# Next MLP block's rows turned from the fifth product on into a third pool of tiles, its sums split into stages, and some evictions and block outputs issued in later steps

## The chip, the cores and the metric

The kernel runs on one core of a Trainium2 chip. The metric is the time on the device in microseconds (us), the median of the runs shown.

## The reference, cut to what matters

The reference is one layer of a hybrid decoder, in float32, for 2048 prompt rows and 64 sample rows of width 1024. A token mixer (attention, a state space model and a short convolution side by side) comes first and is not touched by the change. Behind it stands the MLP:

```python
        h = rms_norm(x, norm_mlp_pre[l])
        f = jnp.square(jax.nn.relu(h @ w_mlp_up[l])) @ w_mlp_down[l]
        x = x + rms_norm(f, norm_mlp_post[l])
```

The first product goes from 1024 to 4096 columns, the second back.

## The kernel before, in words

The MLP stage is the code from line 1566 on; in the profiled execution it runs from about 1345 us to the end of the span. The 2112 rows are done in three blocks of 704 (`BT`), and each block has two halves of 352 rows (`HT`), called t = 0 and 1 where they are read, 1 and 2 where they are written. Rows are cut into three pieces `TP` of 128, 128 and 96.

**Products.** Both matrix products of a block are done by a scheme of the Strassen kind: each is cut in two along rows, inner dimension and columns, and seven products of combined quarters replace eight. `UP_ORDER` is 1, 2, 6, 7, 5, 3, 4 and `DOWN_ORDER` is 1, 2, 7, 4, 5, 6, 3; the numbers name the products, so that "the fifth and sixth product" of the change are the numbers 5 and 6 of the down order. Quarters of the weights were combined earlier and lie in HBM. A product runs over eight steps (`jj`), a step holds two column tiles j. Every operand is split into a high part (a cast to fp32r) and a low part (the rest), and `mm3` issues three matmuls for each pair: high by high, high by low, low by high. An up step has 24 matmuls of 128x352, a down step 18 of 128x512.

**The operands.** The weight of a step is loaded by SyncE's queue (`wraw4`), its high half is made by ScalarE (`whi4`, line 1604), and its low half (`wlo4`) by GpSimd in up steps and by VectorE in down steps (`w_split`). The moving operand is split by `s_pair`: ScalarE makes `shi` (line 1612), VectorE makes `slo`. The pool s4 holds seven such pairs. VectorE's and GpSimd's operations are recorded by a helper, so that all of them have line 137 in the profile; TensorE's have line 118, its transposes 122.

**Inputs of up.** `Half` loads normalised rows (`xt4`) from the scratch xn_d on SyncE's queue, turns them by transposes on TensorE into `pq` banks, and ScalarE copies each with the gain into a `q` tile (line 1638): eight for each half, `q11`, `q12` for the first and `q21`, `q22` for the second, four tiles in each. `up_sums` makes the combined inputs of products 6, 7, 5 and 3 from them on VectorE, four operations for each of four tiles c, three of them TENSOR_TENSOR (`s3` = q11 − q21, then q21 − q22, then q11 becomes q21 − q11) and one SCALAR_TENSOR_TENSOR (q12). It begins when the fourth pair of product 2 has been emitted. `next_block`, a generator that the main loop advances, is started at down product 6, step 2, for the block after.

**Outputs.** `up_out` evicts a bank of an up product on VectorE or ScalarE (line 1701) into the inner tiles `X`, which `relu2` squares on ScalarE (lines 1694, 1695). `down_out` evicts a bank of a down product into the `y1` and `y2` tiles (three operations on a bank in product 6, two in product 5). `square` sums the squares of y on ScalarE (`jkf`, line 1805); `mlp_out` makes the norm's factor (`ssf`, `rstd`) on GpSimd, scales y on VectorE, and adds it to the result by a DMA on GpSimd's queue.

**Order of the work.** The kernel is emitted step by step in the main loop (line 1846 on), but a list scheduler (`schedule_with_timeline_sim=True`) places the instructions on each engine's queue after that, by its own simulated times; only `tc.issue_after(V.last)` pins an operation behind VectorE's last one. Pools of tiles: f4 has 64 of 128x352, r4 8, t4 2.

Of the kernel before, what the change touches and what calls it, by code (L numbers as in the profile page):

```python
# [10 lines left out]
F32 = mybir.dt.float32  # L11
# [3 lines left out]
ALU = mybir.AluOpType  # L15
# [4 lines left out]
P = 128  # L20
# [5 lines left out]
TT = S + TS  # L26
# [17 lines left out]
HT = 352  # L44
BT = 2 * HT
# [99 lines left out]
def hybrid_layer(ctx: ExitStack, tc: tile.TileContext, I, O, stage=9):  # L145
    nc = tc.nc
    V, A, G, PE, SP = Last(nc.vector), nc.scalar, Last(nc.gpsimd), TimedPE(nc.tensor), Last(nc.sync)
# [81 lines left out]
    def sb(name, bufs, side=None):  # L229
        return tc.tile_pool(name=name, bufs=bufs, side=side, reuse_waits="tile")  # L230
# [13 lines left out]
    streams = []  # L244
# [106 lines left out]
    p1l, p1r, p3, p4, psm, ppo = (ExitStack() for _ in range(6))  # L351
# [7 lines left out]
    psT = p4.enter_context(psb("psT", 2))  # L359
# [773 lines left out]
    class Tok:  # L1133
# [436 lines left out]
    e4 = s4 = w4 = r4 = f4 = y4 = t4 = psD = None  # L1570
# [37 lines left out]
    def s_pair(src):  # L1608

        hi = s4.tile([P, HT], F32R, name="shi", tag="s")  # L1610
        lo = s4.tile([P, HT], F32R, name="slo", tag="s")
        A.copy(hi, src)  # L1612
        V.tensor_sub(lo, src, hi.bitcast(F32))
        return hi, lo

    class Half:
# [13 lines left out]
        def turn(self, ps, tag):  # L1630

            self.q = [], []
            for k in range(KC):
                pt = ps.tile([P, 512], F32, name=f"pq{k}", tag=tag)
                for xt, a, n in self.xs:
                    PE.transpose(pt[:, a:a + n], xt[:n, k * P:(k + 1) * P], ident[:n, :n])
                q = (r4 if self.t == 0 else f4).tile([P, HT], F32, name="q", tag="f")
                A.activation(q, pt[:, :HT], AF.Copy, scale=vec[:, V_MLP + k:V_MLP + k + 1])
                self.q[k // 4].append(q)
                yield 1.0  # L1640
# [46 lines left out]
    Y = {}  # L1687

    def f_tile(t, f, j):
        X[t, f, j] = (r4 if (t, f) == (2, 2) and j >= 12 else f4).tile([P, HT], F32, name=f"x{t}{f}", tag="f")  # L1690
        return X[t, f, j]

    def relu2(x, sign):
# [28 lines left out]
    def up_sums(b):  # L1722

        (q11, q12), (q21, q22) = halves[b, 0].q, halves[b, 1].q
        while len(up_s.get((b, 2), [])) < 4:
# [10 lines left out]
        src.update({(b, 6): q11, (b, 7): s3, (b, 5): q21, (b, 3): q12, (b, 4): q22})  # L1736

    src = {}

    def up_split(b, i, cs):  # L1740
        up_s.setdefault((b, i), []).extend(s_pair(src[b, i][c]) for c in cs)

    down_s = {}

# [62 lines left out]
    def mlp_out(b, t, p, last=False):  # L1807
# [14 lines left out]
        for t1, t2 in ((t0, min(t0 + n, S)), (max(t0, S), t0 + n)):  # L1822
            if t1 < t2:
                G.dma_start(y_rows(t1, t2 - t1), y[t1 - t0:t2 - t0], accum_op=ALU.add)

    def second_half(b):

        h = halves[b, 1] = Half(b, 1, XT if b else [(y4, "y")])
        h.rows()
        yield 10.0  # L1830
        yield from h.turn(psT, "tr")
        yield from up_sums(b)

    def next_block(b):
        h = halves[b, 0] = Half(b, 0, XT)
        h.rows()
        yield 16.0
        yield from h.turn(psT, "tr")
# [6 lines left out]
    for at, (kind, b, i, jj) in enumerate(steps):  # L1845
        if at + 4 < len(steps):
            w_load(at + 4)
        while nsplit[0] < len(steps) and nsplit[0] <= at + (2 if idle_y(nsplit[0]) else 1):
            w_split(nsplit[0])
            nsplit[0] += 1  # L1850
        order = UP_ORDER if kind == "u" else DOWN_ORDER
        nxt = steps[at + 2] if at + 2 < len(steps) else None

        if kind == "u" and jj == NJ // 2 - 2 and i != UP_ORDER[-1]:
            ni = UP_ORDER[UP_ORDER.index(i) + 1]
            if ni == 6:
                while (b, 6) not in src:
                    advance(min(streams, key=lambda st: st[1]))
            up_split(b, ni, (0, 1, 2))
        if kind == "d" and i == DOWN_ORDER[-1] and jj == NJ // 2 - 1 and (b + 1, 1) in src:  # L1860
            up_split(b + 1, 1, (0, 1, 2))

        two = steps[at + 1] if at + 1 < len(steps) else None
        if two is not None and two[0] == "d" and kind == "d":
            for j2 in range(2):
                down_split(two[1], two[2], 2 * two[3] + j2)
        if kind == "u":
            hi, lo = wts.pop(at)
            s = up_s[b, i]
            for j2 in range(2):  # L1870
                ps = bank()
                for c in range(4):
                    ws = slice(2 * P * c + P * j2, 2 * P * c + P * j2 + P)
                    mm3(ps[:, :HT], hi[:, ws], lo[:, ws], *s[c], c == 0, c == 3)
                up_out(i, 2 * jj + j2, ps)
        else:
            hi, lo = wts.pop(at)
            if jj == 0:
                banks = [bank() for _ in TP]
            for j2 in range(2):  # L1880
                j = 2 * jj + j2
                s = down_s.pop((b, i, j))
                ws = slice(512 * j2, 512 * j2 + 512)
                for p, (a, n) in enumerate(TP):
                    mm3(banks[p][:n], s[0][:, a:a + n], s[1][:, a:a + n], hi[:, ws], lo[:, ws], j == 0, j == NJ - 1)
            if jj == NJ // 2 - 1:
                for p in range(len(TP)):
                    down_out(i, p, banks[p])
        if two is not None and two[0] == "d" and kind == "u":
            for j2 in range(2):  # L1890
                down_split(two[1], two[2], 2 * two[3] + j2)
        if kind == "u" and jj == NJ // 2 - 1 and i != UP_ORDER[-1]:
            up_split(b, UP_ORDER[UP_ORDER.index(i) + 1], (3,))
        if kind == "d" and i == DOWN_ORDER[-1] and jj == NJ // 2 - 1 and b + 1 < TT // BT:
            while (b + 1, 1) not in src:
                advance(min(streams, key=lambda st: st[1]))
            have = len(up_s.get((b + 1, 1), []))
            up_split(b + 1, 1, range(have, 4))
        if kind == "d":
            end, last = jj == NJ // 2 - 1, b == TT // BT - 1  # L1900
            if i == 2 and end:
                for p in range(len(TP)):
                    square(1, p, 1)
                    if last:
                        o = Y[1, p][:TP[p][1], :512]
                        V.tensor_mul(o, o, g4[:TP[p][1], :512])
            if i == 6 and end:
                for p in range(len(TP)):
                    for d in (1, 2):
                        square(2, p, d)  # L1910
            if i == 3 and not end and 1 <= jj <= len(TP):
                mlp_out(b, 2, jj - 1)
            if i == 3 and end:
                for p in range(len(TP)):
# [48 lines left out]
```

## Time and profile before

| what | value |
|---|---|
| runs | 2792.34, 2794.55 and 2804.75 us, median 2794.55 |
| profiled execution | 2796.83 us, of which the span is 2794.9 |
| mean granted clock of TensorE in it | 0.968 |
| TensorE matmuls busy | 2588.7 us, 93% of the span |
| VectorE, ScalarE, GpSimd busy | 55%, 48%, 39% |

The busy shares are means over the whole program. In the rows of a timeline, the first two numbers are the start and the duration in us, and the brackets hold the idle time of that engine ahead of the row and what ended it. In a group, busy time and the mean in ns stand behind the bar. The clock is a share of full speed.

### The profile page before, as it was taken

Reading aid. Unit: us, or ns where it says so; the run is one execution under the profiler, and the core shown is the slowest. Engines: PE = TensorE matmul, PEld = TensorE weight load, DVE = VectorE, ACT = ScalarE, POOL = GpSimd, SP = SyncE. Lnnn points to the kernel's source line nnn. Section 1 sums busy time; section 2 is a strip of 40 time slices with the busy share of each in tenths; the row PEclk is TensorE's granted clock in tenths of the full one; section 3 lists DMA queues with packets and bytes.
Section 4 is the critical chain, followed back from the end, with each engine's and each line's share of the span. In section 5 each row is a group of like instructions: output and inputs, shape, how many; then the busy total and the mean of one; then the engine's idle time right before and its main releaser. Section 6 shows DMA issues by size and latency. Waiting matters only on the chain. (4 is left out here: it accounts for less than half of the span.)

```text
span 2794.9 us, 40722 instructions
## 1 busy us (share of the span) xinstructions
PE 2588.7 (93%) x14329; PEld 2186.8 (78%) x14329; DVE 1531.4 (55%) x2994; ACT 1327.7 (48%) x2776; POOL 1078.8 (39%) x1008
## 2 busy tenths in 40 slices
PE   7998889999899878999899999999999999999996
PEld 6897777877877755567799877689987779998775
DVE  4555436456456465554164466844546684445676
ACT  4534334435436333334446654453764455385434
POOL 4545445444354543334567300166610016661002
PEclk9999989999999989999999999999999999999998
DMA  7777998777677549878777545574434456443443
GB/s 210 218 185 224 276 254 228 199 218 213 173 207 205 152 149 287 266 227 260 233 233 212 140 157 171 145 218 146 166 128 151 149 146 197 162 163 128 128 146 92
DMA packets 426260, 528.26 MB, mean 189 GB/s; under 512 B 65482, under 2 KB 326130, under 8 KB 421448
## 3 DMA queue, kind: packets, MB, share of 16 engines
q1 hardware_dynamic: 411352, 483.45, 54.5%
q0 software_dynamic: 14704, 42.21, 9.2%
q8 instruction: 113, 1.85, 0.3%
q14 instruction: 91, 0.75, 0.1%
HBM read 447.90 MB, written 178.19 MB: 224 GB/s over the span
## 5 line engine op out<-in xcount | busy, mean ns | idle before, releaser
L137 POOL TENSOR_TENSOR wlo<-wraw,whi 128x512 fp32r<-128x512 f32 (+2 forms) x359 | 670.7, 1899 | 555.0 <-ACT whi L417 288.4
L1604 ACT CAST whi<-wraw 128x1024 fp32r<-128x1024 f32 x336 | 351.7, 1049 | 341.4 <-PE pm L118 274.3
L118 PE MATMUL pm<-slo,whi 128*128 128x352 f32 x1344 | 437.9, 327 | 16.1 <-DVE slo L137 10.0
L118 PE MATMUL pm<-shi,wlo 128*128 128x352 f32 x1344 | 433.1, 328 | 7.6 <-POOL wlo L137 7.5
L118 PE MATMUL pm<-shi,whi 128*128 128x352 f32 x1344 | 438.2, 326 | 0.0
L118 PE MATMUL pm<-wlo,shi 128*128 128x512 f32 (+1 forms) x1008 | 400.1, 397 | 1.9 <-ACT shi L1612 1.7
L118 PE MATMUL pm<-whi,shi 128*128 128x512 f32 (+1 forms) x1008 | 398.4, 395 | 0.0
L118 PE MATMUL pm<-whi,slo 128*128 128x512 f32 (+1 forms) x1008 | 338.1, 399 | 17.6 <-DVE slo L137 17.6
L137 DVE TENSOR_TENSOR wlo<-wraw,whi 128x1024 fp32r<-128x1024 f32 (+1 forms) x169 | 206.2, 1220 | 198.1 <-ACT whi L1604 189.1
L118 PE MATMUL pj<-lo,whi 128*128 128x512 f32 (+1 forms) x720 | 273.1, 380 | 17.0 <-ACT xr L631 8.1
L118 PEld LDWEIGHTS pm<-slo,whi 128*128 128x128 f32 x1344 | 256.0, 191 | 19.9 <-DVE slo L137 11.2
L118 PE MATMUL pj<-hi,whi 128*128 128x512 f32 (+1 forms) x720 | 263.1, 365 | 0.0
L118 PEld LDWEIGHTS pm<-shi,wlo 128*128 128x128 f32 x1344 | 255.1, 191 | 9.2 <-POOL wlo L137 8.9
L118 PE MATMUL pj<-hi,wlo 128*128 128x512 f32 (+1 forms) x720 | 262.1, 365 | 0.0
L137 POOL TENSOR_TENSOR ssf<-ssf 128x1 f32<-128x1 f32 (+1 forms) x18 | 6.6, 369 | 647.1 <-ACT jkf L1805 647.0
L118 PEld LDWEIGHTS pm<-shi,whi 128*128 128x128 f32 x1344 | 256.0, 191 | 0.2
L137 DVE TENSOR_TENSOR x<-pm,x 128x352 f32<-128x352 f32 x240 | 123.4, 521 | 222.5 <-PE pm L118 222.4
L118 PEld LDWEIGHTS pm<-whi,slo 128*128 128x128 f32 (+1 forms) x1008 | 179.7, 181 | 76.0 <-DVE slo L137 26.3
L118 PEld LDWEIGHTS pm<-wlo,shi 128*128 128x128 f32 (+1 forms) x1008 | 182.4, 181 | 60.4 <-ACT shi L1612 8.7
L118 PEld LDWEIGHTS pm<-whi,shi 128*128 128x128 f32 (+1 forms) x1008 | 182.0, 181 | 51.2
L1612 ACT CAST shi<-x 128x352 fp32r<-128x352 f32 x288 | 136.9, 484 | 155.0 <-DVE x L137 102.8
L137 DVE TENSOR_TENSOR slo<-x,shi 128x352 fp32r<-128x352 f32 x288 | 157.1, 554 | 35.6 <-ACT shi L1612 30.5
(324 smaller groups left out, 4887.3 us busy)
## 6 DMA issues: line engine op xcount, KB each, us to landing
wraw<-in_w_in SPq DMA_DIRECT2D x192, 256.0 KB
wraw<-u_d SPq DMA_DIRECT2D x96, 512.0 KB
wraw<-d_d SPq DMA_DIRECT2D x96, 512.0 KB
wraw<-in_w_mlp_up SPq DMA_DIRECT2D x72, 512.0 KB
wraw<-in_w_mlp_down SPq DMA_DIRECT2D x72, 512.0 KB
u_d<-in_w_mlp_up POOLq DMA_DIRECT2D x64, 256.0 KB, 5.6
d_d<-in_w_mlp_down POOLq DMA_DIRECT2D x64, 256.0 KB, 7.3
out_s_k<-in_cache_attn_k SPq DMA_DIRECT2D x8, 2040.0 KB
```

The source lines that it names most:

```text
L118: return self.eng.matmul(out, lhsT, rhs, **kw)
L137: out = f(*args, **kw)
L1604: A.copy(hi, raw)
L1612: A.copy(hi, src)
```

## The change

It does four things, all in the MLP stage.

1. The pool f4 shrinks from 64 to 48 tiles, and a new pool v4 has 16. The second half's `q` tiles come from v4, and so do twelve of the inner tiles X(2,2) (the other four stay in r4).
2. `next_block` starts at down product 5, step 4, and turns the second half ahead of the first.
3. `up_sums` is cut into stages, and `s3` is no longer among them: first q21 − q22, after the pairs of product 1 q11 = q21 − q11, after those of product 2 q12. `s3` is formed in `up_split` just before product 7 splits it, by SCALAR_TENSOR_TENSOR into a t4 tile.
4. At the end of down products 5 and 6 the first bank is evicted at once, the evictions of the second and third (with the squares of y2) go onto a list `late`, of which one is issued in each following step. The finish of y1 at a block's end (square and `mlp_out`) goes onto the same list, except in the last block. `mlp_out` of y2 comes in steps 2 to 4 of product 3 instead of 1 to 3.

```diff
-    f4 = p4.enter_context(sb("f4", 64, "left"))
+    f4 = p4.enter_context(sb("f4", 48, "left"))
+    v4 = p4.enter_context(sb("v4", 16, "left"))
...
-                q = (r4 if self.t == 0 else f4).tile([P, HT], F32, name="q", tag="f")
+                q = (r4 if self.t == 0 else v4).tile([P, HT], F32, name="q", tag="f")
...
-        while len(up_s.get((b, 2), [])) < 4:
-            yield 1.0
-        s3 = []
-        for c in range(4):
-            s3.append(f4.tile([P, HT], F32, name="s3", tag="f"))
-            with tc.issue_after(V.last):
-                V.tensor_sub(s3[c], q11[c], q21[c])
-                V.tensor_sub(q21[c], q21[c], q22[c])
-                V.tensor_sub(q11[c], q21[c], q11[c])
-                V.scalar_tensor_tensor(q12[c], q12[c], -1.0, q11[c], op0=ALU.mult, op1=ALU.subtract)
-            yield 3.0
+        yield from each(lambda c: V.tensor_sub(q21[c], q21[c], q22[c]))
+        while len(up_s.get((b, 1), [])) < 4:
+            yield 1.0
+        yield from each(lambda c: V.tensor_sub(q11[c], q21[c], q11[c]))
+        src.update({(b, 6): q11, (b, 5): q21, (b, 4): q22})
+        while len(up_s.get((b, 2), [])) < 4:
+            yield 1.0
+        yield from each(lambda c: V.scalar_tensor_tensor(q12[c], q12[c], -1.0, q11[c], op0=ALU.mult,
+                                                         op1=ALU.subtract))
...
+            if i == 7:
+                a = t4.tile([P, HT], F32, name="s3", tag="t")
+                V.scalar_tensor_tensor(a, src[b, 6][c], -1.0, src[b, 4][c], op0=ALU.mult, op1=ALU.subtract)
...
     def next_block(b):
-        h = halves[b, 0] = Half(b, 0, XT)
-        h.rows()
-        yield 16.0
-        yield from h.turn(psT, "tr")
-        src[b, 1], src[b, 2] = h.q
-        yield from second_half(b)
+        yield from half(b, 1)
+        yield 6.0
+        yield from half(b, 0)
+        src[b, 1], src[b, 2] = halves[b, 0].q
+        yield from up_sums(b)
...
+        if late:
+            late.pop(0)()
...
                 for p in range(len(TP)):
-                    down_out(i, p, banks[p])
+                    if i in (5, 6) and p:
+                        late.append(lambda i=i, p=p, ps=banks[p]: end_tile(i, p, ps))
+                    else:
+                        end_tile(i, p, banks[p])
...
-        if kind == "d" and i == 6 and jj == 2 and b + 1 < TT // BT:
+        if kind == "d" and i == 5 and jj == 4 and b + 1 < TT // BT:
             stream(next_block(b + 1))
```

What the scheduler makes of it is seen in the queues. Three places follow, all on VectorE, in block 0's down products or block 1's up products.

The end of up product 2 of block 1, before; x11 are evictions of product 2, the q and s3 rows are the sums, and the slo of shi_19108 belongs to the fourth tile of product 6:

```order
L137 TENSOR_TENSOR slo_19031<-q_18102,shi_19030 128x352
L137 TENSOR_TENSOR x11_19007<-pm_18994,x12_18632 128x352
L137 TENSOR_TENSOR s3_19011<-q_18150,q_18638 128x352
L137 TENSOR_TENSOR q_18638<-q_18638,q_18834 128x352
L137 TENSOR_TENSOR q_18150<-q_18638,q_18150 128x352
L137 TENSOR_TENSOR x11_19047<-pm_19034,x12_18675 128x352
L137 SCALAR_TENSOR_TENSOR q_18319<-q_18319,q_18150 128x352
L137 TENSOR_TENSOR x11_19064<-pm_19051,x12_18690 128x352
L137 TENSOR_TENSOR x11_19087<-pm_19074,x12_18717 128x352
L137 TENSOR_TENSOR slo_19109<-q_18150,shi_19108 128x352
```

And with the change, where slo of shi_19103 is that fourth tile's:

```order
L137 TENSOR_TENSOR x11_18925<-pm_18912,x12_18595 128x352
L137 SCALAR_TENSOR_TENSOR q_18397<-q_18397,q_18373 128x352
L137 TENSOR_TENSOR x11_18949<-pm_18936,x12_18617 128x352
L137 TENSOR_TENSOR x11_18966<-pm_18953,x12_18632 128x352
L137 SCALAR_TENSOR_TENSOR q_18403<-q_18403,q_18379 128x352
L137 TENSOR_TENSOR x11_18990<-pm_18977,x12_18654 128x352
L137 TENSOR_TENSOR x11_19007<-pm_18994,x12_18669 128x352
L137 TENSOR_TENSOR x11_19042<-pm_19029,x12_18707 128x352
L137 TENSOR_TENSOR x11_19059<-pm_19046,x12_18722 128x352
L137 TENSOR_TENSOR x11_19082<-pm_19069,x12_18744 128x352
L137 TENSOR_TENSOR slo_19104<-q_18379,shi_19103 128x352
```

The tensor sums have left the place, and one SCALAR_TENSOR_TENSOR (q12) stands for each two evictions; what moved stands at the start of product 1 and of product 2.

The end of down product 6 of block 0, before; y rows are evictions, x12 forms the operands of product 3, and slo of shi_17961 is product 3's first:

```order
L137 TENSOR_TENSOR y2_17150<-pm_17718,y2_17150 128x512 x2
L137 TENSOR_TENSOR y1_16580<-pm_17718,y1_16580 128x512
L137 TENSOR_TENSOR y2_17152<-pm_17719,y2_17152 128x512 x2
L137 TENSOR_TENSOR y1_16582<-pm_17719,y1_16582 128x512
L137 TENSOR_TENSOR y2_17154<-pm_17720,y2_17154 96x512 x2
L137 TENSOR_TENSOR y1_16584<-pm_17720,y1_16584 96x512
L137 TENSOR_TENSOR wlo4_18016<-wraw4_17881,whi4_18015 128x1024
L137 SCALAR_TENSOR_TENSOR x12_14048<-x12_14048,x11_14402 128x352
L137 TENSOR_TENSOR slo_17962<-x12_14020,shi_17961 128x352
```

And with the change, where slo of shi_18006 is product 3's first:

```order
L137 TENSOR_TENSOR y2_17153<-pm_17725,y2_17153 128x512 x2
L137 TENSOR_TENSOR y1_16583<-pm_17725,y1_16583 128x512
L137 TENSOR_TENSOR y2_17155<-pm_17726,y2_17155 128x512 x2
L137 TENSOR_TENSOR y1_16585<-pm_17726,y1_16585 128x512
L137 SCALAR_TENSOR_TENSOR x12_14051<-x12_14051,x11_14399 128x352
L137 TENSOR_TENSOR y2_17157<-pm_17727,y2_17157 96x512 x2
L137 TENSOR_TENSOR y1_16587<-pm_17727,y1_16587 96x512
L137 TENSOR_TENSOR wlo4_18045<-wraw4_17914,whi4_18044 128x1024
L137 SCALAR_TENSOR_TENSOR x12_14087<-x12_14087,x11_14446 128x352
L137 TENSOR_TENSOR slo_18007<-x12_14023,shi_18006 128x352
```

One x12 row has moved ahead of the third bank's evictions, and another ahead of the first slo; no eviction has moved behind that slo.

The end of block 0 and start of up product 1 of block 1, before; slo of shi_18650 belongs to product 2, and the y1 rows are the last evictions of the block:

```order
L137 TENSOR_TENSOR slo_18363<-q_18102,shi_18362 128x352
L137 TENSOR_TENSOR slo_18367<-q_18150,shi_18366 128x352
L137 TENSOR_TENSOR slo_18651<-q_18198,shi_18650 128x352
L137 TENSOR_TENSOR y1_16580<-pm_18029,y1_16580 128x512
L137 TENSOR_TENSOR y1_16582<-pm_18030,y1_16582 128x512
L137 TENSOR_TENSOR y1_16584<-pm_18031,y1_16584 96x512
L137 TENSOR_TENSOR slo_18655<-q_18238,shi_18654 128x352
L137 TENSOR_TENSOR slo_18659<-q_18278,shi_18658 128x352
```

And with the change, where slo of shi_18682 is product 2's:

```order
L137 TENSOR_TENSOR slo_18415<-q_18373,shi_18414 128x352
L137 TENSOR_TENSOR slo_18419<-q_18379,shi_18418 128x352
L137 TENSOR_TENSOR y1_16583<-pm_18066,y1_16583 128x512
L137 TENSOR_TENSOR slo_18683<-q_18385,shi_18682 128x352
L137 TENSOR_TENSOR y1_16585<-pm_18067,y1_16585 128x512
L137 TENSOR_TENSOR y1_16587<-pm_18068,y1_16587 96x512
L137 TENSOR_TENSOR q_17750<-q_17750,q_17912 128x352
L137 TENSOR_TENSOR slo_18687<-q_18391,shi_18686 128x352
```

The first eviction of y1 has moved ahead of product 2's first slo, and the first sum (q_17750) has come in behind the third eviction.

More of the change, by code (lines that the diff above doesn't have):

```diff
@@ L1569, in hybrid_layer @@
     UP_ORDER, DOWN_ORDER = (1, 2, 6, 7, 5, 3, 4), (1, 2, 7, 4, 5, 6, 3)
-    e4 = s4 = w4 = r4 = f4 = y4 = t4 = psD = None
+    e4 = s4 = w4 = r4 = v4 = f4 = y4 = t4 = psD = None
     shifts = [(nm, src, b) for b in range(NB) for nm, src in (("s_k", "cache_attn_k"), ("s_v", "cache_attn_v"))]
@@ L1689, in f_tile @@
     def f_tile(t, f, j):
-        X[t, f, j] = (r4 if (t, f) == (2, 2) and j >= 12 else f4).tile([P, HT], F32, name=f"x{t}{f}", tag="f")
+        pool = f4 if (t, f) != (2, 2) else v4 if j < 12 else r4
+        X[t, f, j] = pool.tile([P, HT], F32, name=f"x{t}{f}", tag="f")
         return X[t, f, j]
@@ L1724, in up_sums, with each @@
         (q11, q12), (q21, q22) = halves[b, 0].q, halves[b, 1].q
+        def each(f):
+            for c in range(4):
+                with tc.issue_after(V.last):
+                    f(c)
+                yield 3.0
+        yield from each(lambda c: V.tensor_sub(q21[c], q21[c], q22[c]))
[3 more added lines that the diff above has]
+        src.update({(b, 6): q11, (b, 5): q21, (b, 4): q22})
         while len(up_s.get((b, 2), [])) < 4:
             yield 1.0
-        s3 = []
-        for c in range(4):
-            s3.append(f4.tile([P, HT], F32, name="s3", tag="f"))
-            with tc.issue_after(V.last):
-                V.tensor_sub(s3[c], q11[c], q21[c])
-                V.tensor_sub(q21[c], q21[c], q22[c])
-                V.tensor_sub(q11[c], q21[c], q11[c])
-                V.scalar_tensor_tensor(q12[c], q12[c], -1.0, q11[c], op0=ALU.mult, op1=ALU.subtract)
-            yield 3.0
-        src.update({(b, 6): q11, (b, 7): s3, (b, 5): q21, (b, 3): q12, (b, 4): q22})
+        yield from each(lambda c: V.scalar_tensor_tensor(q12[c], q12[c], -1.0, q11[c], op0=ALU.mult,
+                                                         op1=ALU.subtract))
+        src[b, 3] = q12
     src = {}
     def up_split(b, i, cs):
-        up_s.setdefault((b, i), []).extend(s_pair(src[b, i][c]) for c in cs)
+        while (b, 6 if i == 7 else i) not in src:
+            advance(min(streams, key=lambda st: st[1]))
+        for c in cs:
+            if i == 7:
+                a = t4.tile([P, HT], F32, name="s3", tag="t")
+                V.scalar_tensor_tensor(a, src[b, 6][c], -1.0, src[b, 4][c], op0=ALU.mult, op1=ALU.subtract)
+            else:
+                a = src[b, i][c]
+            up_s.setdefault((b, i), []).append(s_pair(a))
     down_s = {}
@@ L1824, in mlp_out, with end_tile, half @@
                 G.dma_start(y_rows(t1, t2 - t1), y[t1 - t0:t2 - t0], accum_op=ALU.add)
+    def end_tile(i, p, ps):
+        down_out(i, p, ps)
+        for t, d in {2: [(1, 1)], 6: [(2, 1), (2, 2)]}.get(i, []):
+            square(t, p, d)
+    def half(b, t):
+        h = halves[b, t] = Half(b, t, XT if b else [(y4, "y")])
+        h.rows()
+        yield 12.0
+        yield from h.turn(psT, "tr")
     def second_half(b):
-        h = halves[b, 1] = Half(b, 1, XT if b else [(y4, "y")])
-        h.rows()
-        yield 10.0
-        yield from h.turn(psT, "tr")
+        yield from half(b, 1)
         yield from up_sums(b)
     def next_block(b):
-        h = halves[b, 0] = Half(b, 0, XT)
-        h.rows()
-        yield 16.0
-        yield from h.turn(psT, "tr")
-        src[b, 1], src[b, 2] = h.q
-        yield from second_half(b)
+        yield from half(b, 1)
+        yield 6.0
+        yield from half(b, 0)
+        src[b, 1], src[b, 2] = halves[b, 0].q
+        yield from up_sums(b)
+    late = []
     nsplit = [1]
@@ L1855, in hybrid_layer @@
             ni = UP_ORDER[UP_ORDER.index(i) + 1]
-            if ni == 6:
-                while (b, 6) not in src:
-                    advance(min(streams, key=lambda st: st[1]))
             up_split(b, ni, (0, 1, 2))
@@ L1900, in hybrid_layer, with finish @@
             end, last = jj == NJ // 2 - 1, b == TT // BT - 1
-            if i == 2 and end:
+            if i == 2 and end and last:
                 for p in range(len(TP)):
[L1903 to L1912, printed above, removed]
+                    o = Y[1, p][:TP[p][1], :512]
+                    V.tensor_mul(o, o, g4[:TP[p][1], :512])
+            if i == 3 and not end and 2 <= jj < 2 + len(TP):
+                mlp_out(b, 2, jj - 2)
             if i == 3 and end:
-                for p in range(len(TP)):
+                def finish(p, b=b, last=last):
                     square(1, p, 2)
                     mlp_out(b, 1, p, last)
-        if kind == "d" and i == 6 and jj == 2 and b + 1 < TT // BT:
+                for p in range(len(TP)):
+                    if last:
+                        finish(p)
+                    else:
+                        late.append(lambda p=p, f=finish: f(p))
+        if kind == "d" and i == 5 and jj == 4 and b + 1 < TT // BT:
             stream(next_block(b + 1))
```

1 line of the change is left out of this document (added).

## The prediction

> **What bounds the kernel now.** I read the page first, then the waits of TensorE in the MLP stage, which is the only stage that the change touches (about 1345 us of the span to its end), then windows of 25 us there, and last the timelines of the engines around each hole. The page's first row says what sets the time:
>
> ```profile
> PE 2588.7 (93%) x14329; PEld 2186.8 (78%) x14329; DVE 1531.4 (55%) x2994; ACT 1327.7 (48%) x2776; POOL 1078.8 (39%) x1008
> ```
>
> TensorE is the bound and the change gives it the same matmuls as before. So the time can only change by holes in TensorE, and by the clock after them. Two entries of what TensorE waits for between 1345 and 2795 us:
>
> ```profile
> PE pm L118 <- DVE slo L137: 27.6, 14, 3.7
> PE pq L122 <- DMA xt<-xn_d: 3.6, 3, 2.0
> ```
>
> The 27.6 us are 14 waits for a low half (slo) from VectorE. The windows say where the long holes are (columns: stretch, length, busy time of PE, PEld, DVE, ACT, POOL, granted clock):
>
> ```profile
> 1825.00:1850.00 25.00, 20.55 (x116) 19.46 (x116) 8.15 (x9) 13.15 (x27) 18.26 (x17) 0.93 0.65 160
> 1875.00:1900.00 25.00, 21.15 (x127) 20.56 (x126) 22.67 (x31) 16.39 (x33) 12.50 (x6) 0.97 0.64 219
> 1900.00:1925.00 25.00, 25.00 (x151) 25.00 (x150) 9.21 (x15) 7.31 (x9) 16.79 (x7) 0.96 0.43 139
> 2375.00:2400.00 25.00, 21.33 (x123) 21.28 (x123) 11.09 (x17) 11.01 (x17) 16.50 (x7) 0.93 0.48 158
> ```
>
> I call the sites A (end of down product 5), B (end of down product 6), C (a new block's up product 1) and D (up product 2 into 6). D is the second and third row together (block 1) and the fourth (block 2); C is the first.
>
> **The change part by part.**
>
> *D, the sums leave product 2.* This is the hole in block 1, first TensorE, then VectorE, ScalarE and GpSimd:
>
> ```profile
> 1898.58 0.66 PE L118 MATMUL pm<-slo,whi 128*128 128x352 f32 x1 [3.65 <-DVE slo L137]
> ```
> ```profile
> 1890.09 3.19 DVE L137 TENSOR_TENSOR q<-q 128x352 f32<-128x352 f32 x2
> 1897.04 1.48 DVE L137 TENSOR_TENSOR slo<-q,shi 128x352 fp32r<-128x352 f32 x1 [2.03 <-ACT shi L1612]
> ```
> ```profile
> 1893.75 0.50 ACT L1694 ACTIVATE x<-x 128x352 f32<-128x352 f32 x1 [2.64 <-DVE x L137]
> 1896.54 0.47 ACT L1612 CAST shi<-q 128x352 fp32r<-128x352 f32 x1
> ```
> ```profile
> 1889.88 2.47 POOL L137 TENSOR_TENSOR wlo<-wraw,whi 128x1024 fp32r<-128x1024 f32 x1 [2.37 <-ACT whi L1604]
> ```
>
> Two sums (q from q and q) take 3.19 us, while GpSimd makes a wlo from 1889.88 for 2.47 us. The eviction behind them (x from PSUM) is late, and ScalarE idles 2.64 us for it until 1893.75, works through its ReLUs and a whi, and only at 1896.54 makes the shi of the fourth tile of product 6; VectorE's slo follows, and TensorE has waited 3.65 us. The changed order has a single TENSOR_TENSOR sum left in product 2, near its start, then one SCALAR_TENSOR_TENSOR to each two evictions; of that kind the trace has
>
> ```profile
> L137 DVE SCALAR_TENSOR_TENSOR q<-q 128x352 f32<-128x352 f32 x4 | 2.1, 518 | 0.1
> L137 DVE TENSOR_TENSOR q<-q 128x352 f32<-128x352 f32 x8 | 12.4, 1555 | 0.6 <-DVE s L137 0.5
> ```
>
> that is 0.52 us where the removed kind took 1.56. An eviction then waits for at most one of them. The chain is early by the 3.19 us of the pair and more, which covers the 3.65 to within half a microsecond; that rest lies behind nine matmuls of product 6 that use its first three tiles. Worth: idle 25 − 21.15 = 3.85, and clock (0.03 + 0.04) × 25 = 1.75, together 5.6 in block 1; 3.67 + 0.07 × 25 = 5.4 in block 2. D is **−11.0**, or −5.5 if one of them stays, and not beyond −11.5, since no more than this is idle there. Block 0 never had this hole.
>
> The removed sums do not vanish. They stand in product 1 now, behind the scalings of y1, where VectorE is idle:
>
> ```profile
> 1829.94 5.33 DVE L137 SCALAR_TENSOR_TENSOR y<-y,rstd,gpost 128x512 f32<-128x512 f32 x4 [0.44 <-POOL rstd L137]
> 1862.74 0.53 DVE L137 TENSOR_TENSOR slo<-q,shi 128x352 fp32r<-128x352 f32 x1 [27.48 <-PE pm L118]
> ```
>
> Six tensor sums at 1.56 us, and two s3 and a few slo at about 0.5, are 12 us of 27.48. Here a rule speaks against the change: the Trainium skill, "SBUF — State Buffer", section "SBUF: two separate sides", says that a VectorE operation with two SBUF inputs and a GpSimd operation take a port pair as an exclusive lock, and that whichever comes second is blocked for the whole instruction of the other. The long q sums above agree with it and the 0.52 us of the SCALAR_TENSOR_TENSOR doesn't settle it. By the rule alone every moved sum might cost a wlo pass, and the gain of D would only be kept because the idle stretch is long.
>
> *C, the start of a block.* TensorE, then VectorE, then GpSimd:
>
> ```profile
> 1832.78 0.43 PE L118 MATMUL pm<-shi,wlo 128*128 128x352 f32 x1 [3.67 <-POOL wlo L137]
> 1838.81 0.52 PE L122 MATMUL pq<-cst,xt 128*128 128x128 f32 x3 [0.37 <-ACT q L1638]
> 1839.74 0.43 PE L118 MATMUL pm<-slo,whi 128*128 128x352 f32 x1 [0.41 <-ACT whi L1604]
> ```
> ```profile
> 1819.29 4.46 DVE L137 TENSOR_TENSOR slo<-q,shi 128x352 fp32r<-128x352 f32 x5
> 1823.67 1.87 DVE L137 TENSOR_TENSOR y<-pm,y 128x512 f32<-128x512 f32 x3
> ```
> ```profile
> 1820.70 2.67 POOL L137 TENSOR_TENSOR wlo<-wraw,whi 128x1024 fp32r<-128x1024 f32 x1 [1.72 <-ACT whi L1604]
> 1825.18 0.26 POOL L137 TENSOR_TENSOR ssf<-ssf 128x1 f32<-128x1 f32 x1 [1.82 <-ACT jkf L1805]
> 1826.19 0.28 POOL L137 TENSOR_TENSOR ssf<-ssf 128x1 f32<-128x1 f32 x1 [0.74 <-ACT jkf L1805]
> 1830.40 2.33 POOL L137 TENSOR_TENSOR wlo<-wraw,whi 128x1024 fp32r<-128x1024 f32 x1
> ```
>
> TensorE waits for the third wlo of the block. GpSimd makes it only after the norm of y1, whose queue order the change leaves as it is. That norm starts late because the fifth slo stands in front of the three evictions and is held until GpSimd's second wlo ends at 20.70 + 2.67 = 1823.37. In the changed order the first eviction stands ahead of that slo. So the second and third evictions are the first two after 1823.67 and not the second and third: 1.87 / 3 = 0.6 us earlier, and the square of the first is out of ScalarE's way already. GpSimd has 26.19 − 25.18 = 1.01 us between the first two ssf, a gap that goes if the first square is done early. Between 0.6 and 1.01 I take 0.95, near the gap, since GpSimd's queue behind it runs without a pause. Beside it the transposes and their q leave product 1, and with them the waits of 0.37 and 0.41. That is −1.73 a transition, and there are two: C is **−3.5**. It is 0 if GpSimd's chain keeps its start and ScalarE is as full as now, and −7 if the clock (0.07 × 25 = 1.75 each) comes back too.
>
> *B, the end of down product 6.* The change means to spread nine evictions over three steps. The order says that VectorE's queue still has them all in front of the slo that TensorE needs:
>
> ```profile
> 1789.00 1.46 PE L118 MATMUL pm<-whi,slo 128*128 128x512 f32 x3 [3.65 <-DVE slo L137]
> ```
> ```profile
> 1781.47 5.47 DVE L137 TENSOR_TENSOR y<-pm,y 128x512 f32<-128x512 f32 x9 [0.25 <-PE pm L118]
> 1786.86 1.21 DVE L137 TENSOR_TENSOR wlo<-wraw,whi 128x1024 fp32r<-128x1024 f32 x1
> 1787.99 0.52 DVE L137 SCALAR_TENSOR_TENSOR x<-x,x 128x352 f32<-128x352 f32 x1
> 1788.43 0.52 DVE L137 TENSOR_TENSOR slo<-x,shi 128x352 fp32r<-128x352 f32 x1
> ```
>
> Now: six evictions, one x, three evictions, wlo, x, slo. That is one x more, 88.43 − 87.99 = 0.44 us, in three blocks: B is **+1.3**, between 0 (ScalarE's shi may be what it waits for) and +2.6.
>
> *A, the end of down product 5.*
>
> ```profile
> 1750.62 0.97 PE L118 MATMUL pm<-whi,slo 128*128 128x512 f32 x3 [1.21 <-DVE slo L137]
> 1753.83 0.96 PE L118 MATMUL pm<-whi,slo 128*128 128x512 f32 x3 [0.51 <-DVE slo L137]
> ```
>
> The first slo again has one x more in front (+0.44); the second slo comes before the next wlo instead of after it, so the 0.51 goes. In block 2 two x stand in front (+0.88). Sum **+0.3**, ends −3 (should the evictions really be late) and +2.
>
> *Block 0's sums.* They stay in product 2, eleven operations behind one another after the twelfth eviction, in front of product 6's slo. Before it was
>
> ```profile
> 1418.69 0.43 PE L118 MATMUL pm<-slo,whi 128*128 128x352 f32 x1 [1.24 <-DVE slo L137]
> 1423.65 0.43 PE L118 MATMUL pm<-slo,whi 128*128 128x352 f32 x1 [1.44 <-DVE slo L137]
> ```
>
> I take the same 2.7 us, **0**, with ends −2.7 (both gone) and +3 (one more hole like D's).
>
> *Transposes, their loads and q.* As many as before, and as many loads wait for TensorE to free the rows. SP has the load of w for product 6 behind two of them, but that weight is first used over a hundred matmuls later. **0**, ends −2 and +3.6 (the 3.6 us of xt waits doubled). The y2 blocks that go out a step later, and late handing on of banks, have the whole of product 3 as cover; s3, formed late, replaces a sum that was there: 0.
>
> Sum: −11.0 − 3.5 + 1.3 + 0.3 = **−12.9 us**. The profiled execution took 2796.83 us (a span of 2794.9 and 1.93 around it), 2.3 above the median; it would be 2783.9, and the median of 2794.55 becomes **2781.7**, 0.46% less. About 0.5% (14.0 us, so 2780.6) is what a measurement of this kernel can tell from no change.
>
> **The rivals.**
>
> *Clock regained (0.12).* At C the hole shrinks to 3.67 − 0.95 = 2.7 us. If such a hole no longer halves the clock, two times 1.75 more go: 2778.2. Against it stands a hole at site A of block 2 with a slower pace behind it, and for it the two of 1.24 and 1.44 above, behind which no lower pace stands:
>
> ```profile
> 2706.64 0.99 PE L118 MATMUL pm<-whi,slo 128*128 128x512 f32 x3 [1.89 <-DVE slo L137]
> 2707.43 0.62 PE L118 MATMUL pm<-wlo,shi 128*128 128x512 f32 x1
> 2707.85 0.63 PE L118 MATMUL pm<-whi,shi 128*128 128x512 f32 x1
> ```
>
> 0.42 us from start to start here; so the halving can come after 1.89 us, and I give this little. The Trainium skill, "TensorE: Matmul & The Clock Gate", section "What's actually happening", would have it likelier: it puts the drop at an idle window of about 3.4 us. The row of 1.89 us differs from that rule if the hole is all that counts.
>
> *Deferral works after all (0.05).* If the evictions of the second and third bank do not hold A and B, three times 3.65 and A's 1.7 go beside the clock: about −16, 2766. The order speaks against it: nothing moved behind the slo.
>
> *Gain refilled (0.15).* Two evictions still come late at the end of product 2, behind a stretched slo: D stays, and the time is 2781.7 + 11.0 = 2792.7, no change. For it: slo itself took 1.48 in D.
>
> *Slower (0.08).* The moved sums hold up the start of product 2 instead. In VectorE's new queue the fourth slo of product 2 stands behind two s3, and between it and product 2's first eviction stand one sum and three slo of product 6. Such a run of five takes 1.56 + 4 × 0.52 = 3.6 us undisturbed and 2.67 + 4 × 1.48 = 8.6 us where GpSimd holds up each one (2.67 for a sum is 3.19 − 0.52, 1.48 is D's slo). How late an eviction may be is seen in product 2 of before, where no hole of TensorE answers to this gap between two evictions:
>
> ```profile
> 1883.41 0.52 DVE L137 TENSOR_TENSOR x<-pm,x 128x352 f32<-128x352 f32 x1
> 1887.81 0.51 DVE L137 TENSOR_TENSOR x<-pm,x 128x352 f32<-128x352 f32 x1
> ```
>
> So from 87.81 − 83.41 = 4.4 us on TensorE waits for a bank, and for the fourth slo before it: two holes of D's 5.4 us in each of three blocks, 32 in all, 2781.7 + 32 = 2814. Against it: that takes three or more operations held up in a row, and of the eight sums of the row above the mean was 1.56.
>
> **How the numbers follow.** The forecast has 0.60, by its terms from 2774 to 2790. From 2768 to 2796 lie the forecast, the regained clock and the refilled gain, and the bounds at their ends; left out are the deferral that works, the slower case and the tails, together under 0.2. Faster by over 0.5%: four tenths of the forecast (0.24), most of the regained clock (0.10) and the deferral (0.05), 0.39. Within 0.5%: the rest of the forecast, the refilled gain and 0.02, 0.53. Slower: 0.08.
>
> **What would show it.** D right: no wait over 1 us of TensorE for slo at up product 2 into 6 in blocks 1 and 2, and 25 us windows there at 25.00. C right: the wait for POOL wlo at a block's start near 2.7 instead of 3.67, and no pq in product 1. B right: 4.1 instead of 3.65, three times. The forecast is wrong if B's holes are gone, if D's are there, or if a new wait of over 3 us stands in product 1, 5 or 6.

## The result and the profile after

The changed kernel takes 2782.01 us (median of 5 runs, 2779.39 to 2784.67), the kernel before 2794.55 (5 runs, 2792.34 to 2804.75). The ratio is 0.9948 with a 95% interval of 0.9925 to 0.9971: half a per cent faster, 12.5 us, where 12.9 were forecast.

The profiled execution of the changed kernel is one of 2779.39 us. Its MLP stage started 4.7 us earlier than in the one of before (1341.0 against 1345.7 us), which the change can't have done. So I compare the stage itself, from its first matmul to its last, by windows that end at the switch from 352 to 512 columns and back: three blocks, each up and then down. First the kernel before, then the one after (stretch, length, busy time of TensorE and its matmuls; the rest of each row is not used).

```profile
1345.60:1574.20 228.60, 220.83 (x1348) 218.33 (x1349) 101.07 (x159) 136.85 (x237) 151.53 (x80) 0.99 0.76 222
1574.20:1820.30 246.10, 239.93 (x1036) 182.90 (x1035) 166.08 (x260) 118.72 (x199) 10.72 (x14) 0.99 0.49 155
1820.30:2051.80 231.50, 222.71 (x1363) 220.60 (x1362) 111.03 (x169) 137.74 (x241) 140.89 (x67) 0.99 0.52 164
2051.80:2300.30 248.50, 241.33 (x1040) 184.06 (x1039) 166.19 (x260) 119.18 (x200) 9.90 (x13) 0.99 0.48 150
2300.30:2532.40 232.10, 223.94 (x1364) 222.09 (x1363) 111.18 (x169) 137.59 (x242) 141.09 (x67) 0.98 0.52 165
2532.40:2778.00 245.60, 238.40 (x1009) 181.36 (x1007) 165.32 (x261) 111.86 (x185) 8.28 (x13) 0.99 0.42 130
sum 1432.40, PE 1387.13 PEld 1209.34 DVE 820.87 ACT 761.94 POOL 462.42; mean PE 231.19 PEld 201.56 DVE 136.81 ACT 126.99 POOL 77.07
```
```profile
1341.00:1566.40 225.40, 221.43 (x1350) 219.48 (x1351) 94.19 (x158) 136.14 (x237) 152.62 (x80) 0.98 0.76 225
1566.40:1817.10 250.70, 241.83 (x1058) 185.91 (x1057) 165.96 (x260) 122.28 (x206) 11.49 (x14) 0.99 0.49 156
1817.10:2041.60 224.50, 219.01 (x1345) 218.14 (x1344) 103.19 (x169) 135.55 (x235) 143.40 (x67) 0.98 0.52 165
2041.60:2291.40 249.80, 241.07 (x1052) 185.58 (x1051) 166.04 (x260) 122.32 (x206) 10.67 (x13) 0.99 0.48 149
2291.40:2515.00 223.60, 219.31 (x1345) 218.72 (x1344) 104.70 (x169) 134.81 (x233) 143.64 (x67) 0.98 0.54 171
2515.00:2760.60 245.60, 237.52 (x1010) 181.12 (x1008) 165.20 (x261) 111.97 (x185) 9.04 (x13) 0.99 0.42 130
sum 1419.60, PE 1380.18 PEld 1208.95 DVE 799.29 ACT 763.07 POOL 470.86; mean PE 230.03 PEld 201.49 DVE 133.21 ACT 127.18 POOL 78.48
```

The stage is 1432.4 − 1419.6 = 12.8 us shorter, as much as the two medians differ. TensorE is idle 45.3 us in it before and 39.4 after, 5.9 less, and busy 6.9 us less with as many matmuls. Part of the 6.9 is the clock: a slow pace of matmuls stood behind both holes at D and behind the one at A of block 2, about 1.7 us of loss each, and is gone. But behind C of block 1 and behind B of blocks 0 and 2 it lasts longer than before, and the granted clock of the six parts is 0.98 to 0.99 in both kernels, so the rest of the 6.9 stays unexplained. The up parts are 3.2, 7.0 and 8.5 us shorter, the down parts 4.6, 1.3 and 0 us longer. Some of that is only moved: the counts show 18 and 19 matmuls, six groups of three transposes (the 19th stays open), gone from the later up parts, and 22 and 12 more in the down parts ahead of them. The waits of TensorE in the stage are now (total, times, longest):

```profile
PE pm L118 <- DVE slo L137: 21.3, 11, 4.1
PE pq L122 <- DMA xt<-xn_d: 5.4, 4, 2.1
```

The windows of 25 us at D and C, first D in blocks 1 and 2, then C:

```profile
1875.00:1900.00 25.00, 25.00 (x157) 25.00 (x156) 12.60 (x21) 15.88 (x27) 16.17 (x7) 1.00 0.61 211
2350.00:2375.00 25.00, 25.00 (x158) 25.00 (x157) 12.81 (x21) 14.66 (x25) 16.52 (x7) 1.00 0.46 148
1825.00:1850.00 25.00, 19.51 (x103) 18.64 (x102) 9.11 (x13) 10.48 (x16) 19.45 (x12) 0.86 0.62 146
```

D is full and at full clock. C is not: TensorE is idle 5.5 us there. The window of before has 4.45, but it begins 3 us earlier in the block and so leaves out the last of these waits; over the first 40 us of the block TensorE is idle 4.9 us before and 5.5 after in block 1, 4.4 and 4.3 in block 2. The rows of C in block 1, TensorE, then GpSimd, VectorE and ScalarE:

```profile
1829.03 0.66 PE L118 MATMUL pm<-shi,wlo 128*128 128x352 f32 x1 [3.43 <-POOL wlo L137]
1836.45 0.43 PE L118 MATMUL pm<-slo,whi 128*128 128x352 f32 x1 [0.85 <-ACT whi L1604]
1849.49 0.43 PE L118 MATMUL pm<-slo,whi 128*128 128x352 f32 x1 [1.21 <-ACT whi L1604]
```
```profile
1820.13 0.48 POOL L137 TENSOR_TENSOR ssf<-ssf 128x1 f32<-128x1 f32 x1
1822.06 0.62 POOL L137 TENSOR_TENSOR ssf<-ssf 128x1 f32<-128x1 f32 x1 [1.45 <-ACT jkf L1820]
1826.64 2.33 POOL L137 TENSOR_TENSOR wlo<-wraw,whi 128x1024 fp32r<-128x1024 f32 x1
```
```profile
1821.68 0.51 DVE L137 TENSOR_TENSOR q<-q 128x352 f32<-128x352 f32 x1
1822.11 0.94 DVE L137 TENSOR_TENSOR slo<-q,shi 128x352 fp32r<-128x352 f32 x2
```
```profile
1844.85 1.05 ACT L1604 CAST whi<-wraw 128x1024 fp32r<-128x1024 f32 x1 [2.19 <-DMA wraw<-in_w_mlp_up]
1847.44 2.00 ACT L1604 CAST whi<-wraw 128x1024 fp32r<-128x1024 f32 x2
```

The times are compared by their distance from the block's first matmul (1820.32 before, 1817.10 after). The second ssf has come forward much as forecast: it starts 4.96 us behind that matmul, 5.87 before, 0.91 earlier. But it takes 0.62 us where it took 0.28, and the operation behind it also takes longer (0.35 for 0.19), while VectorE makes the first moved sum and two slo (the rows at 1821.68 and 1822.11). So the third wlo starts 9.5 us behind the first matmul, 10.1 before: 0.5 earlier and not 0.95. Block 2 shows the same durations to within 0.01 us. And where the wait for q and one for whi stood (0.37 and 0.41), one for whi of 0.85 stands; a later one for whi, 0.50 before, is 1.21, and the cast it waits for stands behind one whose weight DMA brought late.

B, the end of down product 6, TensorE, then VectorE, then ScalarE:

```profile
1785.04 1.65 PE L118 MATMUL pm<-whi,slo 128*128 128x512 f32 x3 [4.09 <-DVE slo L137]
```
```profile
1777.08 3.68 DVE L137 TENSOR_TENSOR y<-pm,y 128x512 f32<-128x512 f32 x6 [0.26 <-PE pm L118]
1780.67 0.51 DVE L137 SCALAR_TENSOR_TENSOR x<-x,x 128x352 f32<-128x352 f32 x1
1781.11 1.88 DVE L137 TENSOR_TENSOR y<-pm,y 96x512 f32<-96x512 f32 x3
1782.90 1.21 DVE L137 TENSOR_TENSOR wlo<-wraw,whi 128x1024 fp32r<-128x1024 f32 x1
1784.47 0.95 DVE L137 TENSOR_TENSOR slo<-x,shi 128x352 fp32r<-128x352 f32 x2
```
```profile
1777.57 0.48 ACT L1612 CAST shi<-x 128x352 fp32r<-128x352 f32 x1
```

This is the row order that was forecast and its 0.44 us more: 4.09 for 3.65. ScalarE had the shi of that slo (the cast shown) at 1778.05. So the slo stood in VectorE's queue for 6.4 us with nothing missing.

### The profile page after: what moved, and what is told of

It is laid out like the page before. It is cut to its first block, busy times and chain, and to the rows that moved or that the text cites. A ratio compares the mean times of both kernels' runs of the same rounds, so it can differ in the third digit from the quotient of the medians.

```text
span 2777.6 us, 40701 instructions
## 1 busy us (share of the span) xinstructions
PE 2577.4 (93%) x14329; PEld 2182.4 (79%) x14329; DVE 1509.1 (54%) x2994; ACT 1328.9 (48%) x2776; POOL 1087.9 (39%) x1008
```

## The experiments

Each kernel ran beside the kernel before on the same chip. The ratios are those of this pairing; the last column is the MLP stage of one profiled execution.

| kernel | median, us | ratio to before, 95% interval | stage, us |
|---|---|---|---|
| before | 2794.55 | | 1432.4 |
| changed | 2782.01 | 0.9948, 0.9925 to 0.9971 | 1419.6 |
| sums back in product 2 | 2787.06 | 0.9967, 0.9952 to 0.9981 | 1424.35 |
| nothing late | 2774.12 | 0.9940, 0.9917 to 0.9964 | 1413.5 |
| evictions pinned | 2760.84 | 0.9892, 0.9876 to 0.9907 | 1398.2 |
| sums alone | 2789.79 | 0.9983, 0.9967 to 0.9999 | 1422.4 |
| sums and start alone | 2784.88 | 0.9955, 0.9936 to 0.9974 | 1418.2 |
| one wlo on VectorE | 2779.77 | 0.9948, 0.9931 to 0.9966 | 1414.8 |
| three wlo on VectorE | 2783.71 | 0.9949, 0.9931 to 0.9966 | 1421.2 |
| pinned, three wlo | 2762.57 | 0.9882, 0.9854 to 0.9910 | 1397.8 |
| pinned, three wlo, copies earlier | 2761.11 | 0.9856, 0.9839 to 0.9872 | 1393.1 |
| pinned, copies earlier | 2758.85 | 0.9847, 0.9832 to 0.9861 | 1392.3 |

The kernel before took 2793.55 to 2801.26 us in the median beside them, so that medians of different rows are compared by their ratios. The stage is of a single execution and counts for less: for "sums back" it is the slowest of ten executions (2793.85 us), for "sums alone" and "sums and start alone" the fastest of ten (2780.58 and 2774.75).

**Sums back in product 2.**

```diff
-        yield from each(lambda c: V.tensor_sub(q21[c], q21[c], q22[c]))
-        while len(up_s.get((b, 1), [])) < 4:
-            yield 1.0
-        yield from each(lambda c: V.tensor_sub(q11[c], q21[c], q11[c]))
         while len(up_s.get((b, 2), [])) < 4:
             yield 1.0
+        for c in range(4):
+            with tc.issue_after(V.last):
+                V.tensor_sub(q21[c], q21[c], q22[c])
+                V.tensor_sub(q11[c], q21[c], q11[c])
+                V.scalar_tensor_tensor(q12[c], q12[c], -1.0, q11[c], op0=ALU.mult, op1=ALU.subtract)
+            yield 3.0
...
```

> The changed kernel with the sums of up products 6, 5 and 3 formed together again, after the fourth pair of product 2, on VectorE (two TENSOR_TENSOR and one SCALAR_TENSOR_TENSOR for each tile; s3 stays late). Theory (the gain is the sums that left product 2): holes of TensorE for slo come back between up product 2 and 6 of blocks 1 and 2, of 1 to 3.7 us each, and with the clock 6 to 11 us: 2788 to 2793 where the changed kernel has 2782. Rival 1 (the deferred evictions and block outputs bring the gain): 2782, no such hole. Rival 2 (the earlier turning, which takes transposes and q out of product 1, brings it): 2782.

The ratio went up from 0.9948 to 0.9967, with intervals that overlap; the stage is 4.8 us longer in an execution 6.8 us above its median, which doesn't tell the two apart either. No wait for slo came back at D. There is one for GpSimd's wlo in each of blocks 1 and 2 (1.18 and 1.36 us); in block 1:

```profile
1892.48 0.43 PE L118 MATMUL pm<-shi,wlo 128*128 128x352 f32 x1 [1.18 <-POOL wlo L137]
```

So the sums may stand in product 2, as long as they start with it; in this kernel the last sum stands nine evictions ahead of the fourth slo of product 6 on VectorE's queue, in the kernel before two. What D needed was not that the sums leave product 2, but that they end well before it does. My theory was too narrow there.

**Sums alone**, that is the staged `up_sums` and `up_split` of the changed kernel, put into the kernel before.

> The kernel before with the staged sums and the late s3 alone; the pools, the start of the turning, its order and the evictions as before. Theory (the sums must leave product 2, and for that the second half must be turned before product 1): the second half's q come during product 1 and 2, the sums of four tiles bunch up at the end of product 2, and the holes there stay or grow: 2790 to 2797. Rival (taking s3 out and staging is what counts, wherever the sums stand): the holes of 3.65 go, 2783 to 2785.

2789.79 us; the two holes of 3.65 shrank and stayed:

```profile
1889.30 0.43 PE L118 MATMUL pm<-slo,whi 128*128 128x352 f32 x1 [1.13 <-DVE slo L137]
2362.54 0.43 PE L118 MATMUL pm<-slo,whi 128*128 128x352 f32 x1 [1.64 <-DVE slo L137]
```

Ahead of the first of them VectorE does the sums in a bunch near product 2's end; five of them:

```profile
1880.41 4.48 DVE L137 TENSOR_TENSOR q<-q 128x352 f32<-128x352 f32 x5
```

The bunching was expected; the holes, which I expected to stay whole or grow, shrank. Staging and the later s3 together take 4.55 of the 7.32 us of the two waits away; which of the two does it was not tried.

**Sums and start alone**: the same, and the next block's turning begun earlier.

```diff
-        if kind == "d" and i == 6 and jj == 2 and b + 1 < TT // BT:
+        if kind == "d" and i == 5 and jj == 4 and b + 1 < TT // BT:
```

> The kernel before with the staged sums, late s3 and the start of the next block's turning at down product 5, step 4; pools, the order of the halves and all evictions as before. Theory (these two parts are the gain of the change): no hole over 1 us for slo between up product 2 and 6 in blocks 1 and 2, 10 to 14 us less than before: 2780 to 2784. Rival (the third pool or the second half's going first is needed): as with the staged sums alone, holes of 1.1 to 1.6 us there, 2788 to 2791.

Its ratio of 0.9955 and its stage of 1418.2 us are the changed kernel's within what these can tell. No wait for slo is left at D; block 1 has one of 1.93 us in the fifth step of product 2, for an eviction behind sums that VectorE took 2.08 to 2.75 us over. So these two parts bring the gain of the change, as far as such intervals can tell: the third pool, the second half's going first and the late evictions aren't needed for it. Beside "sums alone" it shows that the earlier start takes away what was left of the holes. The earlier start alone, with the sums of the kernel before, was not tried.

**Nothing late**: the two `late.append` taken out, evictions, squares and block outputs issued at once.

> The changed kernel with all evictions, squares and block outputs issued at the product's end again, nothing in the list of late work. Theory: the deferral moved nothing behind the slo that TensorE waits for and only put one more x in front of it; without it the waits at the end of down product 6 are 3.65 again instead of 4.1, 1.3 us less in all, up to 3 with the clock: 2779 to 2782. Rival 1 (the deferral brings the gain): 8 us or more are lost, 2790 or above.

The ratio is 0.9940, not told apart from the changed kernel's 0.9948. The stage is 6.1 us shorter, and the waits say where most of it lies: A's are 0.8 us less in all, B is back at

```profile
1784.52 1.65 PE L118 MATMUL pm<-whi,slo 128*128 128x512 f32 x3 [3.65 <-DVE slo L137]
```

and the wait for loads of rows (xt) is 3.5 us in the stage instead of 5.4. The rival, that the late list brings the gain, falls: without it nothing was lost.

**Evictions pinned behind slo.** The list stays; each bank's evictions are tied to the last slo emitted, and a late bank is issued after the operands of its step.

```diff
+        slo[0] = V.last
         return hi, lo
...
-        down_out(i, p, ps)
+        with tc.issue_after(slo[0]):
+            down_out(i, p, ps)
```

> The changed kernel with each bank's evictions pinned on VectorE's queue behind the last slo that was emitted, the first bank behind the slo of the next product's first step, the second and third one step later each. Theory (VectorE's queue order alone makes the holes at the ends of down products 5 and 6, since shi is there early): the three holes of 4.1 us and their 1.75 of slow clock go, and 1.6 to 2.3 at three ends of product 5; VectorE is full by 0.8 us more than a step for three steps, so 1 to 2 us of each come back: 12 to 20 us less, 2762 to 2770. Rival (the next product can't start without the banks, or shi is late too): the holes stay within half a microsecond, 2780 to 2784.

2760.84 us, 0.9892 of before, below the forecast's lower end. TensorE's waits for slo fell from 21.3 to

```profile
PE pm L118 <- DVE slo L137: 3.9, 8, 1.0
```

and at B the same engine does the same work in another order, with TensorE going on through it:

```profile
1780.78 0.52 DVE L137 TENSOR_TENSOR slo<-x,shi 128x352 fp32r<-128x352 f32 x1
1781.22 1.88 DVE L137 TENSOR_TENSOR y<-pm,y 128x512 f32<-128x512 f32 x3
```

So VectorE's queue order made the holes A and B: with another order the banks don't hold TensorE up there, and the backlog that I feared did not cost anything that shows. The edit ties the evictions of all seven down products, not of 5 and 6 alone.

**One and three wlo of a block's start on VectorE.**

```diff
-        (G if steps[at][0] == "u" else V).tensor_sub(lo, raw, hi.bitcast(F32))
+        (G if steps[at][0] == "u" and not (steps[at][1] and steps[at][2] == 1 and steps[at][3] in (2, 3, 4))
+         else V).tensor_sub(lo, raw, hi.bitcast(F32))
```

> The changed kernel with one wlo at each block's start (the third step of up product 1 in blocks 1 and 2) made by VectorE and not by GpSimd. The block's start kept its wait of 3.43 us for this wlo where I forecast 2.7. Theory 1 (GpSimd's whole queue is late there: behind this wlo stand three output DMAs that wait for VectorE's scalings, and then the next wlo): the wait moves to the fourth step's wlo, 2 to 4 us long, time 2779 to 2784. Theory 2 (this one wlo behind the norm's chain is all): the wait and its slow clock go, 3.4 + 1.75 less 1 to 2 for VectorE's own wait for the first scaling, twice: 2773 to 2776.

> The same with three wlo of that product (third to fifth step) made by VectorE. Theory 1: only now does the start of blocks 1 and 2 get short, 3.4 + 1.75 less 1 to 2 each: 2773 to 2777. Theory 2: as with one. Rival to both (the weights' loads or ScalarE's whi are as late): waits for whi of 2 to 4 us take the place, 2779 to 2784.

With one (the list is `(2,)`), the wait of 3.43 for this wlo fell to 1.32, now for VectorE, and the next wlo took its place, as theory 1 has it:

```profile
1839.65 0.43 PE L118 MATMUL pm<-shi,wlo 128*128 128x352 f32 x1 [3.54 <-POOL wlo L137]
```

With three, that one went too, and the rival came true, a wait for whi behind a late load:

```profile
1850.79 0.66 PE L118 MATMUL pm<-slo,whi 128*128 128x352 f32 x1 [3.93 <-ACT whi L1604]
```
```profile
1848.39 1.04 ACT L1604 CAST whi<-wraw 128x1024 fp32r<-128x1024 f32 x1 [7.98 <-DMA wraw<-in_w_mlp_up]
```

Neither is told apart from the changed kernel (0.9948, 0.9949). At a block's start three things end within a few microseconds of each other: GpSimd's queue, VectorE's, and the weights.

**Pinned with three wlo, and the copies.**

> The evictions pinned behind slo and the three wlo on VectorE together. If the two holes are independent the gains add: 2761 of the pinned kernel less what the three wlo brought to the changed one, 2752 to 2757. If VectorE is then too full at a block's start, 2760 or more.

> Pinned evictions and three wlo on VectorE, and the sixteen 2 MB copies of the caches (out_s_k, out_s_v on SyncE's queue) issued ten steps earlier each, so that none is issued in the last steps ahead of block 1's start or within block 2's product 1. With the wlo on VectorE the wait at a block's start had moved to whi, behind weight loads that landed late (4.2 and 4.6 us). Theory A (the copies delay these loads): the two waits for whi go or fall under 1 us, 5 us each with the clock: 2750 to 2755. Theory B (the block's own output additions and its weight loads fill the DMA engines there, with a share near 1): the waits stay, 2759 to 2765.

> Pinned evictions and the copies ten steps earlier, wlo as in the changed kernel. Theory A: the 0.85 and 1.2 us waits for whi at a block's start go, the wait for GpSimd's wlo of 3.3 stays: 2756 to 2760. Theory B: no difference from the pinned kernel, 2758 to 2764.

The edit of the copies is `at % 20 == 0` for `at % 20 == 10`. The three wlo add nothing to the pinned kernel (0.9882 against 0.9892); the whi waits of its block starts are 4.2 and 4.6 us. With the copies earlier they are still 3.2 and 3.7, so theory A is not borne out. The trace fits theory B: from 1826 to 1841 us of that kernel, ahead of the late weight at block 1's start, the 16 DMA engines are full (shares of 0.97, 1.01 and 0.99 in steps of 5 us), and GpSimd's queue, on which the block's output additions run, has over half of their time (queue q0, whose 1.44 MB are the three additions of 512, 512 and 384 KB; q1 is that of the loads):

```profile
q0 software_dynamic: 400, 1.44, 56.6%
q1 hardware_dynamic: 2015, 2.00, 42.0%
```

No run took the output additions away from there. The copies seem to have cost something elsewhere: the waits for rows, 5.6 us in the pinned kernel, are

```profile
PE pq L122 <- DMA xt<-xn_d: 2.6, 4, 1.7
```

with the copies earlier, and the stage is 5.9 us shorter (4.7 with the three wlo). These are single executions, and the kernels of each pair ran on different chips. The kernel with pinned evictions and copies earlier is the fastest, 0.9847 of before (0.9832 to 0.9861). Its interval lies well clear of the changed kernel's.

## Why the prediction was right, and where it was not

- **D, forecast −11.0.** Both holes are gone, and the windows read 25.00 at a clock of 1.00. By the starts of TensorE's rows, the stretch from the 289th to the 433rd matmul of the up part, which holds D, takes 23.1 us in block 1 for 29.0 and 23.2 in block 2 for 29.0: 11.7 in all. The reason that I gave was half right: the sums were in the way, but the experiments show that the earlier start of the turning lets them end in time, whether they then stand in product 1 or 2. The step that a SCALAR_TENSOR_TENSOR costs 0.52 where a TENSOR_TENSOR costs 1.56 was wrong as a property of the kind; the rows in the last section turn it round.
- **C, forecast −3.5.** This step failed. The evictions and the second ssf came forward by the time that was forecast, but GpSimd's queue behind them did not run on as it had: two of its operations took 0.5 us more in all beside VectorE's first moved sum and slo, and the third wlo came 0.5 us earlier and not 0.95. That the sums cause it is not shown by a run of its own. The waits of 0.37 and 0.41 for q and whi went, and a wait of 0.85 for whi came in each block, in block 1 also 1.21 for 0.50. By the windows, the up parts of blocks 1 and 2 are 15.5 us shorter; about 3 of these are transposes that moved (12 groups of three; behind the one at 1863.91 us of before the next matmul starts at 1864.16, 0.25 us later), D is 11.7, and about 0.8 are left for C. The wlo experiments show why it was hard to gain there: behind each wait stands the next.
- **B, forecast +1.3.** 4.09, 4.12 and 4.08 for 3.65, 3.68 and 3.65: 1.3 us.
- **A, forecast +0.3.** The first wait rose to 1.64 in block 0, as worked out, and the one behind it went. In blocks 1 and 2 it is 2.32, where 1.66 and 2.77 were due; the sum of these waits rose by 0.9.
- **Block 0, forecast 0.** Its up part is 3.2 us shorter. The two waits of 1.24 and 1.44 became three of 0.35, 0.26 and 0.92, which is 1.15 less, and the waits for rows there fell from 2.04 and 0.59 to 0.69. Such waits differ from run to run (in this part 0.7 to 2.4 us in the kernels that turn as this one does); what the change has to do with them was not tried.
- **Loads of rows, forecast 0 between −2 and +3.6.** 5.4 for 3.6 us, within the bounds: less in block 0's up part, more in the down parts, where the turning now begins.

So that the total was hit so closely is luck. C fell short by 2.7 us, and A and the row loads cost 0.6 and 1.8 more than forecast; against them stand 3.2 us in block 0 that I had at zero, 0.7 more at D, and the slow pace behind A of block 2, which went without a term for it (about 1.7). These overlap, the row loads with block 0 above all, and were not taken apart further. D, on which the sign hung, was right. Of the rivals, the regained clock could not come, as C's hole stayed at 3.43; the gain was not refilled; the sums did not hold up product 2. The deferral didn't work, as the order said, and the pinned kernel shows what evictions that are really late bring: 21 us of the stage against the changed kernel, where about 16 had been reckoned.

## What to carry to other kernels

Read the queue, not the source: work that is issued later in the program can still stand ahead of the operand that the bound engine waits for, and a queue row with its operands ready and its consumer idle, as the slo at B, was the cheapest gain here. Tie the filler behind the operand explicitly. Where several queues meet, as at a block's start here, take one wait away and look which comes next before counting its price as a gain.

## What the runs showed of the hardware

VectorE and GpSimd hold each other up in both directions. At D of the kernel before it is VectorE that pays: its two q sums take 3.19 us from 1890.09 on, beside a wlo that GpSimd began at 1889.88. In the changed kernel VectorE began its run of moved q sums first; they take 0.51 us each, and GpSimd's wlo beside them takes 4.43 us, where one alone takes 2.40. Behind the five sums come two s3, until 1834.55, 2.24 us before the end of that wlo, about the time of one alone:

```profile
1831.43 2.25 DVE L137 TENSOR_TENSOR q<-q 128x352 f32<-128x352 f32 x5
```
```profile
1832.36 4.43 POOL L137 TENSOR_TENSOR wlo<-wraw,whi 128x1024 fp32r<-128x1024 f32 x1
```

In product 2 a SCALAR_TENSOR_TENSOR is the second to come, and takes 1.92 us where 0.52 is the rule; the first of the two wlo began at 1864.13:

```profile
1864.13 5.10 POOL L137 TENSOR_TENSOR wlo<-wraw,whi 128x1024 fp32r<-128x1024 f32 x2 [6.27 <-ACT whi L1604]
```
```profile
1865.02 1.92 DVE L137 SCALAR_TENSOR_TENSOR q<-q 128x352 f32<-128x352 f32 x1
```

Between these two kinds, both with two inputs in SBUF here, the kind does not decide; who comes second does. That the one that starts first keeps the shared port pair and the other is blocked is what the Trainium skill says ("SBUF — State Buffer", section "SBUF: two separate sides"), and these rows agree with it.

The length of a hole does not alone decide about the clock either. Behind the changed kernel's waits of 2.32 us matmuls follow at 0.22 us, at full pace, while behind the 1.89 of before they came at 0.42:

```profile
2222.04 0.96 PE L118 MATMUL pm<-whi,slo 128*128 128x512 f32 x3 [2.32 <-DVE slo L137]
2222.84 0.39 PE L118 MATMUL pm<-wlo,shi 128*128 128x512 f32 x1
2223.06 0.39 PE L118 MATMUL pm<-whi,shi 128*128 128x512 f32 x1
```

In the kernel with the sums back in product 2, the hole at A is 2.32 us in both blocks 1 and 2; behind the one of block 1 matmuls follow at 0.23 us, behind the one of block 2 at 0.43:

```profile
2702.27 1.35 PE L118 MATMUL pm<-whi,slo 128*128 128x512 f32 x3 [2.32 <-DVE slo L137]
2703.42 0.63 PE L118 MATMUL pm<-wlo,shi 128*128 128x512 f32 x1
2703.85 0.63 PE L118 MATMUL pm<-whi,shi 128*128 128x512 f32 x1
```

The Trainium skill ("TensorE: Matmul & The Clock Gate", section "What's actually happening") describes a window that runs on by itself, so that where a hole falls in it would matter; no run here set such a window apart from other causes. The holes of 3.4 us and more in the changed kernel were all followed by the slow pace.
